# A two-layer decoder trunk on one core: the first loads of x and of the weights put on one DMA queue in the order of their use

## The chip, the core and the metric

The kernel runs on one core of a Trainium2 chip, in one launch. The metric is the time of one execution on the device in microseconds (us); less is better.

## The reference, cut to what matters

The reference is a decoder trunk of two layers (DEPTH = 2) on a sequence of 256 tokens with 1024 features, in float32. Each layer normalises x, projects it once, feeds the parts to three groups of heads, gates their outputs, and adds one output projection to x:

```python
for l in range(DEPTH):
    h = rms_norm(x, g_pre[l])
    u = h @ w_in[l]
    (qa, ka, va, ga, qb, kb, vb, gb, rb, qm, gm) = jnp.split(u, split_idx, axis=-1)
    oa = merge_heads(moba_attention(qa_h, ka_h, split_heads(va, A_HEADS))) * jax.nn.silu(ga)
    ob = merge_heads(rms_norm(ob, g_gla_out[l])) * jax.nn.silu(gb)
    mkv = rms_norm(mem, g_mem[l]) @ w_mem_kv[l]
    om = merge_heads(mem_attention(qm_h, mk_h, split_heads(mv, M_HEADS))) * jax.nn.silu(gm)
    x = x + jnp.concatenate([oa, ob, om], axis=-1) @ w_out[l]
```

Group A is causal attention with eight heads, group B a chunked gated linear attention (GLA) with four heads, group M attention into 256 memory tokens with four heads. (The lines that make `qa_h`, `ob` and the like are left out here.)

## The kernel before, in words

**Tiling.** x is kept with its features on the 128 partitions: 8 k tiles of 128 x 256. All weights come from DRAM in granules of 8 k tiles of 256 columns (1 MB). Each fp32 operand is split into a high part in the matmul's format (`whi`, `xh`, `oh`, made by ScalarE or GpSimd) and the rest (`wlo`, `xl`, `ol`, made by VectorE), and each product is three matmuls: high by high, and the two mixed ones (L990 to L1005). So ScalarE and VectorE have to split every weight before TensorE can use it.

**The order of the work.** The program is written by a small planner (`Plan`, L47). Every chain of work is a Python generator that asks for an engine, a planned cost and a time before which it can't start; the planner always takes the operation that can start first by its own clock, and the instructions are recorded on each engine in that order. On the chip they run in this order on each engine, each waiting for its inputs. The planner's clock needs to be told when loads land: that is what the numbers in `LANDS` (L36) do. They cause no wait themselves; they decide only in which order the engines' instructions are written. A change in them shifts the choices that come behind.

**The first unit.** The first granules of layer 0 (`vr` and `kq`: values and gate rank, keys and queries of group B) come as one array of 528 columns for each k tile. `start_loads` (L321) issues the loads of x and of these weights in five pieces (`CHUNKS`, L35): k tile 0, k tile 1, then 2 and 3, 4 and 5, 6 and 7. For each piece it issues x on SyncE's queue (L331) and then the weights (L332), on ScalarE's queue for k tiles 0 and 1 and on SyncE's for the rest. `first_x` (L377) splits x, `first_w` (L340) splits the weights (L345 on ScalarE, L347 on VectorE), and `first_sq` (L382) squares and sums x for the norm (L309, L314, L317). `main` (L1032) issues 5 matmuls on zeros ahead of all (`WARM`, L1035), and `first_unit` (L1130) then runs 12 matmuls for each k tile, 6 of 272 columns and 6 of 256.

**Behind it.** `loader` (L353) issues one granule after the other on SyncE's queue, each into one of three raw buffers; the first weights take two of the three and give them back when the last `wlo` of the first unit is done (L351). `split` (L389) makes `whi` (L404) and `wlo` (L406) in four parts of two k tiles, in one of two buffers. Layer 0 then runs the units `ga0`, `va0 va1`, `qa0 ka0`, `mk mv`, `qm`, ... (L25); a unit of two names is done with matmuls of 512 columns (L1005). The unit `mk mv` needs the split memory tokens (`oh`, `ol`) and is led on TensorE by the sum of their squares (L438 over `sqs`, which VectorE adds up in L314 and L317). Between the matmuls of the units stand those of the heads: L880 (logits), L932 (transposes), L947 (probabilities by values), L502 (head norms), and L614 to L732 (GLA). The output projection is matmuls of L998 with `oh` and `ol` in a fixed order of k tiles (`KORD`, L27: 6, 7, 1, 0, 2, ... in layer 0; k tiles 2 and 3 are the last four heads of group A).

Of the kernel before, what the change touches and what calls it, by code (L numbers as in the profile page):

```python
# [16 lines left out]
P = 128  # L17
L = 2
KT = 8
T = 256  # L20
EPS = 1e-6
NPRM = 23
# [6 lines left out]
PAIRK = 0  # L29
SPLIT = 6  # L30
MEMPRIO = 6
WARM = 5
FSQ = 6
STATS = 800
CHUNKS = ((0, 1), (1, 2), (2, 4), (4, 6), (6, 8))  # L35
LANDS = ((3000, 4200), (4300, 4900), (5600, 6800), (7400, 8500), (9200, 10300))  # L36
NB = 528
ENTER, LEAVE, CROSS = 89.0, 189.0, 60.0
SLACK, HOLD = 300.0, 600.0
# [128 lines left out]
def trunk(ctx, tc, xp_d, w0_d, memT_d, wvr_d, win_d, wmkv_d, wout_d, wup_d, cst_d, nb_d, out_d):  # L168
    nc = tc.nc
# [4 lines left out]
    plan = Plan()  # L174
# [15 lines left out]
    xp = big([L * NPRM + KT * T], "xp")  # L190
# [44 lines left out]
    def op(eng, cost, after=0.0, prio=None, table=None, mode="full"):  # L235
        return ("op", [(eng, cost)], after, prio, table, mode)
# [84 lines left out]
    def start_loads():  # L321
        S.activation(warm, ones, AF.Exp)
        got, t0 = yield ("acq", raws, 2)
        raw, hi, lo = (x.rearrange("p a b -> p (a b)")[:, :KT * NB].rearrange("p (k n) -> p k n", n=NB)
                       for x in (raw_t[:, 0:2], whi, wlo))
        done[0, "vk"] = (hi, lo)
        src = w0_d.rearrange("p (k n) -> p k n", n=NB)
        for c, (a, b) in enumerate(CHUNKS):
            tx, tw = LANDS[c]
            xs = slice(L * NPRM + a * T if a else 0, L * NPRM + b * T)  # L330
            nc.sync.dma_start(xp[:, xs], xp_d[:, xs])  # L331
            (nc.scalar if b <= 2 else nc.sync).dma_start(raw[:, a:b], src[:, a:b])  # L332
            plan.spawn(first_x(a, b, tx), 30 - 2 * a)
            plan.spawn(first_w(a, b, tw, raw, hi, lo, got), 29 - 2 * a)
        plan.spawn(first_sq(), 5)
        nc.sync.dma_start(cst, cst_d)
        cst_ev.set(12300)
        nc.sync.dma_start(wup, wup_d)

    def first_w(a, b, t, raw, hi, lo, got):  # L340
# [33 lines left out]
    cst_ev = ev()  # L374
    sq0 = []

    def first_x(a, b, t):  # L377
        for k in range(a, b):
            t1 = yield from split_x(xT, 0, 0, xh, xl, k, t, 30 - 2 * a)
            xev[0][k].set(t1)  # L380
# [649 lines left out]
            wrel[l, nm][k // 2].set(t)  # L1030

    def main():  # L1032
        yield op("P", 4300, 0.0, None, None, "main")
        for j in range(WARM):
            TE.matmul(banks.slots[7][2][:, 0:256], lhsT=zero[:, 0:128], rhs=zero, start=True, stop=True)  # L1035
        idx = {(l, n): i for i, (l, n, _, _) in enumerate(seq)}
        for l in range(L):
# [5 lines left out]
            for unit in UNITS[l] if l == 0 else ("vr", "kq", *UNITS[l]):  # L1043
# [8 lines left out]
                t = 0  # L1052
# [6 lines left out]
                for k, m in order:  # L1059
                    tw = 0  # L1060
                    for x in names:
                        tx = yield ("wait", wts[l, x][k])
                        tw = max(tw, tx)
                    tx = yield ("wait", aev[k])
# [190 lines left out]
```

## Time and profile before

| | us |
|---|---|
| median of three runs | 282.81 |
| the three runs | 282.83, 282.81, 280.1 |
| the profiled execution | 281.19 |
| its span in the profile | 279.4 |

The profile comes from the one profiled execution; its span is 1.79 us shorter than that execution's time. All times below are counted from the start of the span. PE is TensorE's matmuls, DVE is VectorE, ACT is ScalarE, POOL is GpSimd, SP is SyncE; a q behind a name is the engine's own queue of instructions that issue DMAs or wait. A matmul's duration in the profile is that from its start until its results are out, so two neighbours overlap; the step from one start to the next is what a matmul costs.

### The profile page before, as it was taken

To read this page: it belongs to the slowest core of one execution; us is meant where nothing else is said; L and a number is where in the kernel's file an instruction comes from. 1 tells how busy PE (TensorE), PEld (TensorE's weight loads), DVE (VectorE), ACT (ScalarE), POOL (GpSimd) and SP (SyncE) were. 2 spreads that over 40 slices of the span, in tenths; PEclk is the share of its full clock that TensorE was granted. 3 is DMA by queue.
4 is the path that set the end of the run, shared out by engine and by line. 5 is a ranking of instruction groups with operands and counts; after the bars stand their busy time and mean duration, and the time that the engine had idled before them with its cause. 6 is when DMAs were issued, how large, how long until landed. Compare 5 with 4: busy or idle time off the path is not lost.

```text
span 279.4 us, 5773 instructions
## 1 busy us (share of the span) xinstructions
PE 272.0 (97%) x2138; PEld 241.1 (86%) x2138; DVE 229.5 (82%) x568; ACT 193.3 (69%) x430; POOL 89.0 (32%) x111
## 2 busy tenths in 40 slices
PE   8899999799999999999999999999999999999994
PEld 7799788487999997999999886789887888989994
DVE  2899799999888898978999798979986787898631
ACT  4874888777797776967773888759787745956400
POOL 3303394160426424400063318213243730510000
PEclk9999999999999999999999999999999999999999
DMA  7999408560734314343545745228233424151111
GB/s 224 402 361 380 175 0 308 198 246 1 289 107 189 103 72 151 122 168 126 201 160 158 287 151 199 104 82 325 63 135 110 192 108 196 50 196 59 56 56 40
DMA packets 8413, 45.76 MB, mean 164 GB/s; under 512 B 945, under 2 KB 2369, under 8 KB 3393
## 3 DMA queue, kind: packets, MB, share of 16 engines
q1 hardware_dynamic: 8096, 44.85, 43.6%
q10 hardware_dynamic: 288, 0.54, 0.7%
q8 instruction: 17, 0.28, 0.4%
q14 instruction: 12, 0.09, 0.1%
HBM read 44.34 MB, written 1.05 MB: 162 GB/s over the span
## 4 chain that ended last, share of the span: by engine, by line
PE 87%; DVE 7%; DMA 2%; ACT 1%; issue 1%
PE bank L998 49%; PE bank L1005 21%; PE bank L947 4%; PE bank L932 3%; PE bank L880 3%; DVE wlo L406 2%; DMA raw<-w_dram 2%; PE bank L502 2%; DVE ol L301 1%; PE bank L732 1%; PE bank L621 1%; DVE sqs L317 1%; ACT L539 0%; PE bank L530 0%; DVE el L581 0%
## 5 line engine op out<-in xcount | busy, mean ns | idle before, releaser
L406 DVE TENSOR_TENSOR wlo<-raw,whi 128x512 fp32r<-128x512 f32 (+1 forms) x144 | 97.8, 700 | 12.0 <-ACT whi L404 10.1
L404 ACT ACTIVATE whi<-raw 128x512 fp32r<-128x512 f32 (+1 forms) x144 | 86.4, 625 | 24.3 <-PE bank L998 11.3
L998 PE MATMUL bank<-xh,whi 128*128 128x256 f32 x160 | 47.1, 294 | 0.0
L998 PE MATMUL bank<-xl,whi 128*128 128x256 f32 x160 | 44.6, 279 | 0.0
L998 PE MATMUL bank<-xh,wlo 128*128 128x256 f32 x160 | 44.6, 279 | 0.0
L917 POOL TENSOR_SCALAR pe<-pe,rc 128x256 f32<-128x256 f32 (+1 forms) x48 | 29.4, 626 | 35.4 <-DVE rc L914 35.2
L998 PE MATMUL bank<-oh,whi 128*128 128x256 f32 x128 | 35.8, 280 | 0.0
L998 PE MATMUL bank<-ol,whi 128*128 128x256 f32 x128 | 35.7, 279 | 0.0
L998 PE MATMUL bank<-oh,wlo 128*128 128x256 f32 x128 | 35.7, 279 | 0.0
L482 POOL TENSOR_TENSOR cc<-ss,nhalf 128x8 f32<-128x8 f32 x12 | 20.5, 1717 | 45.4 <-DVE ss L480 40.9
L1005 PE MATMUL bank<-whi,xh 128*128 128x512 f32 x80 | 32.9, 411 | 0.0
L1005 PE MATMUL bank<-wlo,xh 128*128 128x512 f32 x80 | 31.4, 393 | 0.0
L998 PEld LDWEIGHTS bank<-xh,whi 128*128 128x128 f32 x160 | 30.2, 189 | 1.4 <-issue 1.0
L1005 PE MATMUL bank<-whi,xl 128*128 128x512 f32 x80 | 31.3, 392 | 0.0
L998 PEld LDWEIGHTS bank<-xl,whi 128*128 128x128 f32 x160 | 30.2, 189 | 0.1
L998 PEld LDWEIGHTS bank<-xh,wlo 128*128 128x128 f32 x160 | 30.1, 188 | 0.0
L998 PE MATMUL bank<-whi,xh 128*128 128x256 f32 (+1 forms) x96 | 28.6, 298 | 0.5 <-ACT whi L345 0.5
L998 PE MATMUL bank<-wlo,xh 128*128 128x256 f32 (+1 forms) x96 | 27.6, 288 | 0.5 <-DVE wlo L347 0.4
L998 PE MATMUL bank<-whi,xl 128*128 128x256 f32 (+1 forms) x96 | 27.3, 284 | 0.0
L998 PEld LDWEIGHTS bank<-oh,whi 128*128 128x128 f32 x128 | 24.3, 190 | 0.2 <-issue 0.2
L998 PEld LDWEIGHTS bank<-ol,whi 128*128 128x128 f32 x128 | 24.0, 188 | 0.0
L998 PEld LDWEIGHTS bank<-oh,wlo 128*128 128x128 f32 x128 | 24.0, 188 | 0.0
(188 smaller groups left out, 608.7 us busy)
## 6 DMA issues: line engine op xcount, KB each, us to landing
raw<-win_dram SPq DMA_DIRECT2D x23, 1024.0 KB, 5.3
raw<-wout_dram SPq DMA_DIRECT2D x8, 1024.0 KB, 4.8
raw<-wmkv_dram SPq DMA_DIRECT2D x4, 1024.0 KB, 4.8
raw<-memT_dram SPq DMA_DIRECT2D x2, 1024.0 KB, 4.8
raw<-w_dram SPq DMA_DIRECT2D x3, 528.0 KB, 8.0
raw<-wvr_dram SPq DMA_DIRECT2D x1, 1088.0 KB, 4.9
nb<-nb_dram SPq DMA_DIRECT2D x1, 1024.0 KB, 8.4
out_dram<-xp SPq DMA_DIRECT2D x8, 128.0 KB, 1.9
```

The costliest lines, as they stand in the source:

```text
L301: V.scalar_tensor_tensor(lo[:, k], src[:, k], col(l, g0 + k), hi[:, k].bitcast(F32), op0=ALU.mult, op1=ALU.subtract)
L317: V.tensor_tensor(sqs, sqs, sq[:, j], op=ALU.add)
L404: S.activation(hi[:, cs], raw[:, cs], AF.Copy)
L406: V.tensor_sub(lo[:, cs], raw[:, cs], hi[:, cs].bitcast(F32))
L482: G.tensor_tensor(c, ss, nhalf, op=ALU.pow)
L502: TE.transpose(ps[:, m, tt * P:tt * P + P], n[:, tt, m * P:m * P + P], ident)
L880: TE.matmul(bk[hh][2][:, a:b], lhsT=x[ds], rhs=y[ds], start=(j == 0), stop=(j == len(prs) - 1))
L917: G.tensor_scalar(pe[:, hh, a:b], pe[:, hh, a:b], rc[:, hh, qt:qt + 1], 1.0, op0=ALU.mult, op1=ALU.mult)
L932: TE.transpose(bk[0][2][:, dst:dst + P], pe[:, hh, src:src + P], ident)
L947: TE.matmul(po[64 * hh:64 * hh + 64, q0:T], lhsT=vv[:, j, c:c + 64], rhs=pt[:, hh, 256 * j:256 * j + T - q0], start=(j == 0), stop=(j == 1))
L998: TE.matmul(ps, lhsT=a, rhs=b, start=(first and j == 0), stop=(lastk and j == 2))
L1005: TE.matmul(ps, lhsT=a, rhs=b, start=(first and j == 0), stop=(lastk and j == 2))
```

## The change

The table of the first loads is written as eleven entries in the order of their use, each with x or w, its k tiles and the time at which the planner takes it as landed. All are issued on SyncE's queue. The weights of k tiles 2 and 3 become two transfers of 264 KB (one of 528 KB before). The planner's landing times are later than before (12100 for the last weights, 10300 before), as are two other numbers of its clock (the constants at 12800, the matmuls on zeros until 4700), and there are 6 matmuls on zeros.

```diff
-WARM = 5
+WARM = 6
 FSQ = 6
 STATS = 800
-CHUNKS = ((0, 1), (1, 2), (2, 4), (4, 6), (6, 8))
-LANDS = ((3000, 4200), (4300, 4900), (5600, 6800), (7400, 8500), (9200, 10300))
+LOADS = (("x", 0, 1, 3100), ("w", 0, 1, 4300), ("x", 1, 2, 4600), ("w", 1, 2, 5300), ("x", 2, 4, 6000),
+         ("w", 2, 3, 6700), ("w", 3, 4, 7600), ("x", 4, 6, 8300), ("w", 4, 6, 9900), ("x", 6, 8, 10600),
+         ("w", 6, 8, 12100))
...
-        for c, (a, b) in enumerate(CHUNKS):
-            tx, tw = LANDS[c]
-            xs = slice(L * NPRM + a * T if a else 0, L * NPRM + b * T)
-            nc.sync.dma_start(xp[:, xs], xp_d[:, xs])
-            (nc.scalar if b <= 2 else nc.sync).dma_start(raw[:, a:b], src[:, a:b])
-            plan.spawn(first_x(a, b, tx), 30 - 2 * a)
-            plan.spawn(first_w(a, b, tw, raw, hi, lo, got), 29 - 2 * a)
+        for what, a, b, t in LOADS:
+            if what == "x":
+                xs = slice(L * NPRM + a * T if a else 0, L * NPRM + b * T)
+                nc.sync.dma_start(xp[:, xs], xp_d[:, xs])
+                plan.spawn(first_x(a, b, t), 30 - 2 * a)
+            else:
+                nc.sync.dma_start(raw[:, a:b], src[:, a:b])
+                plan.spawn(first_w(a, b, t, raw, hi, lo, got), 29 - 2 * a)
...
-        cst_ev.set(12300)
+        cst_ev.set(12800)
...
-        yield op("P", 4300, 0.0, None, None, "main")
+        yield op("P", 4700, 0.0, None, None, "main")
```

The lines of the changed kernel stand one or two further down than those of the kernel before (L404 becomes L406, L998 becomes L1000).

SyncE's queue at the program's start, before (`xp` is x with the small parameters, `raw` the weights as loaded, `w_dram` the first weights, 528 columns for a k tile); the weights of k tiles 0 and 1 stand on ScalarE's queue:

```order
L331 DMA xp<-xp_dram 128x302
L331 DMA xp<-xp_dram 128x256
L331 DMA xp<-xp_dram 128x512
L332 DMA raw<-w_dram 128x1056
L331 DMA xp<-xp_dram 128x512
L332 DMA raw<-w_dram 128x1056
```

and now:

```order
L332 DMA xp<-xp_dram 128x302
L335 DMA raw<-w_dram 128x528
L332 DMA xp<-xp_dram 128x256
L335 DMA raw<-w_dram 128x528
L332 DMA xp<-xp_dram 128x512
L335 DMA raw<-w_dram 128x528 x2
L332 DMA xp<-xp_dram 128x512
```

The weights of k tiles 0 and 1 have moved in between the pieces of x, ahead of x of k tiles 2 and 3.

VectorE around the first parts of `mk` and `mv`, before (`wlo` is the low part of a weight granule, `sqs_130` the sum of the memory tokens' squares, `el`, `ee` and `wz` are GLA's; counted from layer 0's first granule, the 21st `wlo` is the first row that reads `wlo` here, and the 24th is the second of the four in the last):

```order
L406 TENSOR_TENSOR wlo<-raw,whi 128x512
L581 TENSOR_TENSOR el_132<-b 128x32x4
L317 TENSOR_TENSOR sqs_130<-sqs_130,sq_103 128x256
L601 TENSOR_TENSOR el_131<-el_131,kf 128x8x16
L583 TENSOR_TENSOR el_132<-b 128x32x4
L406 TENSOR_TENSOR wlo<-raw,whi 128x512
L317 TENSOR_TENSOR sqs_130<-sqs_130,sq_103 128x256
L601 TENSOR_TENSOR el_131<-el_131,kf 128x16x8
L581 TENSOR_TENSOR el_132<-b 128x64x2
L406 TENSOR_TENSOR wlo<-raw,whi 128x512 x4
```

and now, from the 21st `wlo` to the 24th, which is the first of the last row:

```order
L408 TENSOR_TENSOR wlo<-raw,whi 128x512
L666 TENSOR_TENSOR wz_133<-qf,ee 128x128
L595 TENSOR_TENSOR wz_134<-el_131,qf 128x128
L318 TENSOR_TENSOR sqs_130<-sqs_130,sq_103 128x256
L302 SCALAR_TENSOR_TENSOR ol<-raw,xp,oh 128x256
L408 TENSOR_TENSOR wlo<-raw,whi 128x512
L670 TENSOR_TENSOR ee<-ee,kf 128x128
L595 TENSOR_TENSOR wz_134<-el_131,qf 128x128
L408 TENSOR_TENSOR wlo<-raw,whi 128x512
L444 TENSOR_SCALAR vx_610<-bank_99 128x2
L408 TENSOR_TENSOR wlo<-raw,whi 128x512 x3
```

The last sum of squares now stands ahead of the 22nd `wlo` (ahead of the 23rd before), and GLA's L601 and the `el_132` rows have moved behind.

TensorE at the start of the unit `mk mv`, before (`sqs_130` as above, `zl` and `ee` are GLA's, `oh` and `ol` the split memory tokens):

```order
L1005 MATMUL bank_99<-whi,xl 128x512
L679 MATMUL bank_92<-zl_135,ee 128x512
L438 MATMUL bank_94<-ones,sqs_130 128x1 x2
L1005 MATMUL bank_95<-whi,oh 128x512
L1005 MATMUL bank_95<-wlo,oh 128x512
```

and now:

```order
L1007 MATMUL bank_97<-whi,xl 128x512
L440 MATMUL bank_99<-ones,sqs_130 128x1 x2
L1007 MATMUL bank_94<-whi,oh 128x512
L1007 MATMUL bank_94<-wlo,oh 128x512
L1007 MATMUL bank_94<-whi,ol 128x512
```

GLA's matmul L679 has moved into the unit, 37 rows further down on TensorE. From the last part of layer 0's output projection on (the last 1113 of TensorE's 1933 instructions, the last 297 of VectorE's 570 and the last 199 of ScalarE's 386) the order is the same in both kernels.

## Rows read from the trace of the kernel before

**Rows 1.** The page, busy time: engine, busy us, share, instructions.

```profile
PE 272.0 (97%) x2138; PEld 241.1 (86%) x2138; DVE 229.5 (82%) x568; ACT 193.3 (69%) x430; POOL 89.0 (32%) x111
```

**Rows 2.** Who waited for whom, PE alone: us in total, times, longest.

```profile
PE bank L438 <- DVE sqs L317: 1.0, 1, 1.0
PE bank L1005 <- DVE wlo L406: 0.7, 1, 0.7
```

**Rows 3.** The chain that ended last, first 20 us: start us, us, what.

```profile
1.59 5.94 DMA raw<-w_dram
...
8.23 0.80 DVE wlo L347
...
9.08 1.73 PE bank L998 x12
```

**Rows 4.** The timeline of PE, first unit: start us, us, engine, line, instruction.

```profile
5.24 0.79 PE L998 MATMUL bank<-whi,xh 128*128 128x272 f32 x1
5.83 0.43 PE L998 MATMUL bank<-wlo,xh 128*128 128x272 f32 x1
6.06 0.43 PE L998 MATMUL bank<-whi,xl 128*128 128x272 f32 x1
...
7.39 0.28 PE L998 MATMUL bank<-xl,whi 128*128 128x256 f32 x1
7.51 0.28 PE L998 MATMUL bank<-xh,wlo 128*128 128x256 f32 x1
...
19.56 0.50 PE L438 MATMUL bank<-ones,sqs 128*128 128x1 f32 x4
```

**Rows 5.** Line L1035, the matmuls on zeros: durations in ns, first and last start.

```profile
L1035 PE MATMUL bank<-ob x10: 634/634/795, 1.2 to 5.2; 128*128 128x256 f32 x10
```

**Rows 6.** The timeline of the queues that issue the first loads.

```profile
1.18 0.86 ACTq L332 DMA_DIRECT2D raw<-w_dram  x2
...
9.44 6.72 SPq L362 DMA_DIRECT2D raw<-win_dram  x3
```

**Rows 7.** Stretches: per engine us busy; then PEclk, DMA share, GB/s.

```profile
2.00:4.00 2.00, 2.00 (x6) 1.55 (x6) 0.26 (x1) 0.72 (x3) 0.83 (x6) 1.00 0.97 274
4.00:8.00 4.00, 3.79 (x17) 3.22 (x15) 1.44 (x4) 1.58 (x4) 0.01 (x1) 1.00 1.00 342
8.00:12.00 4.00, 3.30 (x22) 2.88 (x23) 3.77 (x8) 3.99 (x9) 1.97 (x3) 1.00 1.05 410
```

**Rows 8.** The timeline of ACT and DVE where the last first weights are split.

```profile
13.08 1.18 ACT L345 ACTIVATE whi<-raw 128x528 fp32r<-128x528 f32 x2 [0.33 <-DMA raw<-w_dram]
...
14.49 1.31 DVE L347 TENSOR_TENSOR wlo<-raw,whi 128x528 fp32r<-128x528 f32 x2
```

**Rows 9.** The timeline of PE at the start of the unit mk mv.

```profile
49.10 1.02 PE L679 MATMUL bank<-zl,ee 128*128 128x512 f32 x2
51.16 0.60 PE L438 MATMUL bank<-ones,sqs 128*128 128x1 f32 x4 [1.03 <-DVE sqs L317]
51.62 0.47 PE L1005 MATMUL bank<-whi,oh 128*128 128x512 f32 x1
52.76 0.50 PE L1005 MATMUL bank<-wlo,oh 128*128 128x512 f32 x1 [0.67 <-DVE wlo L406]
```

**Rows 10.** The chain that ended last, in the same place.

```profile
50.76 0.34 DVE sqs L317
51.10 0.20 DVE el L601
...
51.50 1.21 DVE wlo L406 x2
```

**Rows 11.** The timeline of PE and DVE at the end of layer 0.

```profile
121.60 0.87 PE L947 MATMUL bank<-pts,va 128*64 128x256 f32 x8
...
123.43 0.42 DVE L852 TENSOR_TENSOR ol<-of,oh 128x256 fp32r<-128x256 f32 x1 [0.15 <-ACT oh L850]
...
124.57 0.28 PE L998 MATMUL bank<-oh,whi 128*128 128x256 f32 x1
```

## The prediction

> **What bounds the kernel now.** I read the page first: TensorE's matmuls are busy in 97% of the span, VectorE in 82% [rows 1]. Time can be won only where TensorE stands still or runs slowly, so I next read who makes it wait. Behind the first unit there are two such waits: 1.0 us for a sum of squares (L317) and 0.7 us for a `wlo`, once each [rows 2]. The chain that ended last shows the other place: it begins with the weights of k tile 1, which land 5.94 us after their issue, and goes over their `whi` and `wlo` (8.23 to 9.03) to the matmul at 9.08 [rows 3]. The timeline shows the size: the first unit starts at 5.24, its first 12 matmuls are issued by 7.51, and then almost nothing runs until 9.08; the unit is over at 19.56 [rows 3, 4]. From there TensorE is fed until the unit `mk mv`. There it could have gone on at 50.13 (51.16 less the wait of 1.03), but waits for `sqs`, and then until 52.76 for a `wlo` [rows 9]; the chain runs over VectorE alone there [rows 10]. So there are two places, the first k tile and the start of `mk mv`, and the second belongs to VectorE's arrears. Everything behind layer 0 stands in the same order before and after and reads as busy; I leave it as it is.
>
> **The change part by part.**
>
> *One queue.* Before, the weights of k tiles 0 and 1 are issued by ScalarE's queue at 1.18 [rows 6] and run beside what SyncE's queue has sent. Now 0.83 MB (x and weights of k tiles 0 and 1: 128 partitions x (302 + 256 + 2 x 528) x 4 bytes) stand ahead of everything else. By the rates [rows 7], 0.55 MB are moved between 2 and 4 us, and the other 0.28 MB take 0.8 us at 342 GB/s: 4.8. From the last byte to its use there lies at most 1.9 us: all first loads are 3.24 MB, by the same rows they are through at 11.2, and ScalarE takes up the last at 13.08 [rows 8]. So the weights of k tile 1 can be used at 6.7 at the latest, their `whi` is there at 7.4 and `wlo` at 8.1 (0.65 and 0.80 in the chain, overlapping by little).
>
> *The first unit.* A sixth matmul on zeros puts the first real one off by (5.24 - 1.2) / 5 = 0.8 us [rows 4, 5], to 6.05. Its twelve matmuls take 0.23 from start to start until shortly before 7 (5.83 to 6.06) and 0.12 after it (7.39 to 7.51). The clock column says 1.00 (2.4 GHz) for both [rows 7], so it doesn't explain the change, and I take it by its place: three steps of 0.23 and nine of 0.12 end at 7.8. Bounds: all fast 7.5, all slow 8.8. Without a wait for k tile 1 the other 84 matmuls take 84/83 of the 10.48 from 9.08 to 19.56, so 10.6: the unit ends at 18.4 instead of 19.56, **1.1 us** earlier. The cover: weights of k tiles 4 and 5 end the first 2.43 MB, moved by 9.2 and usable by 11.1; TensorE needs them at 7.8 + 4 x 1.5 = 13.8 less the splits (1.3). For k tile 6 it is 13.08 + 1.25 against 15.3. If the cover goes, each microsecond of a late landing beyond it costs one.
>
> *Two transfers instead of one.* SyncE has three more issues, at 0.4 each (0.86 for ScalarE's two, [rows 6]); the queue runs far ahead of the data, so I take nothing. Bounds: 0 and 1.2 us on everything behind. The rows of those weights are half as long; the rate in the stretch of short ones is 274 GB/s, in that of long ones 410 [rows 7]. The nearest rows are those of 4 to 8 us at 342, where both run. I take the last landing as it is, 13.08, because the bytes are the same and the queue for them too.
>
> The Trainium skill speaks against this edit: its page "DMA: Bandwidth & Descriptors", section "Bandwidth", says to gather transfers to 1 MB or more, with 341 GB/s measured at 1 MB and 138 at 64 KB. The trace agrees as far as its stretches of smaller and larger transfers go (274 and 410 GB/s). By the rule the loads would run at the lower of the rates, which is the slower rival below; by the row of 4 to 8 us they keep their time.
>
> *VectorE up to `mk mv`.* The last first weights are taken up at 13.08; their first `whi` is there at 13.7 (half of 1.18 later) and now nothing stands in VectorE's way: both `wlo` are done at 13.7 + 1.31 = 15.0, against 15.8 [rows 8]: 0.8 earlier. From the last two L347 to the 24th `wlo` (the first of `mv`) VectorE has 79 instructions now, 89 before: three sums of squares went ahead, into time in which it waited (0.34 each), eight of GLA went behind (L581, L583, L593, L601, L670, 0.20 each), one of 0.1 came in [rows 10]: 1.0 + 1.6 - 0.1 = 2.5. So the 24th `wlo` comes 3.3 earlier than 52.71 [rows 10], at 49.4.
>
> *TensorE at `mk mv`.* The GLA matmul at 49.10 [rows 9] now comes later, inside the unit. TensorE is at the sum of squares at 49.10 - 1.1 = 48.0; that sum is ready (it stands ahead of the 22nd `wlo`). It starts `mk mv` at 48.4 (51.16 to 51.62 before) and needs the 24th `wlo` at 48.7, but gets it at 49.4. So it goes on at 49.4 instead of 52.76, 3.3 earlier, and still has the moved matmul to do, which took 1.03 (49.10 to 50.13): **2.3 us** in all, of which 1.1 is the start. Bounds here: 0, if VectorE's lead goes into new waits on the way (only the longest single wait of its kind, 1.03, is then lost again), and 0.7 more, if the `wlo` is in time.
>
> *The end of layer 0.* Two pairs of heads of the last four now finish side by side, with L947 after 18 matmuls of the output projection, and 6 of them ahead of the first use of the first pair's output. Before, one pair has 18 behind it: L947 ends at 122.4, `ol` at 123.85, and its first use is at 124.57 [rows 11]. The chain of 1.45 is now covered by the second pair's L947 (0.8) and six matmuls (0.7), and for the second pair by twelve (1.4). I take 0; bounds -0.3 (TensorE's order has eight groups of matmuls fewer in layer 0) and +1.4 (a chain uncovered).
>
> **The sum.** 281.19 - 2.3 = 278.9 from the profiled execution. It lies 1.6 below the median of the runs; the mean of the four known times is 281.7, and I set the forecast against that: **279.4 us**, 0.8% less.
>
> **The rivals.**
>
> *More.* VectorE's arrears melt further and the `wlo` is there when TensorE wants it: 2.3 + 0.7 + 0.3 = 3.3, so 278.4. For it speaks that three places of VectorE's work went into idle time; against it, that ScalarE has the same table loads and splits to do.
>
> *The start alone.* The 1.1 is won, but the new order of layer 0 gives the rest back, at `mk mv` or in the uncovered chain at the layer's end: between 281.7 - 1.1 = 280.6 and, with the 1.4 of the bound, 282.0. For it speaks that TensorE reads as 97% busy and VectorE has hardly any slack in 15 to 53 us; against it, that VectorE has 2.5 us less to do ahead of the place that waits.
>
> *Slower.* The one queue carries the pieces of 128 to 528 KB at the 274 GB/s of the first stretch [rows 7]. Then 3.24 MB take 11.8 us from 2.0 on and the last weights are usable at 15.7 instead of 13.1. K tile 6 waits 1.2 and the first unit ends at 19.6, no earlier than before. The next granule, which stands behind on the same queue [rows 6], is usable 3.9 later, at 19.6, and split at 20.9: TensorE waits again for 1.2. VectorE is some 3.6 later than forecast, the 24th `wlo` comes at 53.0, and the moved GLA matmul follows: 281.7 + 1.3 = 283.0. From a landing of the last weights at about 14.8 on, the change loses. Against it speaks that six of the eight k tiles were on this queue before too.
>
> *It doesn't do what it says.* The first weights could land no earlier because what holds them up is not the other queue. Then k tile 1 is waited for as before and the sixth matmul on zeros only fills the wait: 281.7 less what VectorE's new order gives, about 280.5.
>
> **How the numbers follow.** The forecast has 0.50, more 0.18, the start alone 0.18, slower 0.07, no earlier landing 0.07. One per cent is 2.8 us, about what a measurement of this kernel can tell from no change. Faster by over that: the rival "more" and some 4 in 10 of the forecast's own spread (the bounds of the first k tile and of `mk mv`, about 1 us to each side), 0.38. Slower by over 1% needs the slower rival with the uncovered chain on top: 0.05. The rest, 0.57, is within. The range reaches from 277.0 (the larger gain, on an execution as short as the profiled one with a further 0.9) to 281.9 (the start alone); what is left out is the slower rival and the last edge of "more".
>
> **What would show it.** Right: the first real matmul at about 6.1 with no gap between k tiles 0 and 1, the first unit over at 18.4, `mk mv` going on at 49.4, and the last 157 us of the span as long as before. Wrong: ScalarE taking up the last first weights later than 14; a wait of more than 1 us at `mk mv` or ahead of L998 at the end of layer 0; a step of 0.23 between matmuls beyond 7 us.

## The result and the profile after

| | before | after |
|---|---|---|
| median of the comparison, 22 executions each | 280.97 | 282.62 |
| lowest to highest | 280.1 to 282.83 | 280.9 to 284.32 |
| profiled execution / its span | 281.19 / 279.4 | 283.19 / 281.3 |

The changed kernel takes 1.0053 of the time before, with an interval of 1.0032 to 1.0074: 1.5 us more. The forecast was 279.4, the range ended at 281.9; sign and range were both missed. Three executions of the experiments below took 537.93, 541.5 and 685.29 us and are left out of all ratios and counts as slow.

The page and the waits of TensorE, of the changed kernel, answer to [rows 1, 2]:

```profile
PE 273.8 (97%) x2140; PEld 242.2 (86%) x2140; DVE 228.9 (81%) x571; ACT 193.0 (69%) x427; POOL 88.5 (31%) x111
```

```profile
PE bank L1007 <- DVE wlo L408: 1.8, 1, 1.8
PE bank L1037 <- DVE ones L1167: 1.2, 1, 1.2
PE bank L1000 <- DVE wlo L349: 0.5, 2, 0.3
PE bank L440 <- DVE sqs L318: 0.3, 1, 0.3
```

TensorE is busy 1.8 us longer with the same matmuls and one more on zeros, and the two waits that should have shrunk (1.0 and 0.7) have become 0.3 and 1.8. A longer busy time for the same work asks for the clock. Stretches of the changed kernel (columns as in [rows 7]; the seventh is the granted clock):

```profile
2.00:4.00 2.00, 2.00 (x6) 1.55 (x6) 0.48 (x1) 0.71 (x2) 0.83 (x6) 1.00 0.94 296
4.00:8.00 4.00, 3.66 (x20) 3.09 (x18) 2.01 (x5) 2.60 (x6) 0.63 (x1) 1.00 0.92 295
8.00:12.00 4.00, 3.82 (x29) 3.61 (x30) 4.00 (x9) 3.13 (x7) 1.66 (x2) 1.00 1.02 363
50.00:52.00 2.00, 0.21 (x2) 0.07 (x1) 2.00 (x7) 2.00 (x7) 2.00 (x2) 1.00 0.70 180
52.00:54.00 2.00, 2.00 (x7) 1.64 (x8) 2.00 (x4) 1.27 (x3) 2.00 (x3) 0.74 1.04 381
54.00:56.00 2.00, 2.00 (x6) 1.52 (x6) 2.00 (x6) 0.00 (x0) 0.73 (x1) 0.50 0.87 352
56.00:58.00 2.00, 2.00 (x10) 1.61 (x9) 1.35 (x6) 0.75 (x2) 1.89 (x2) 0.91 1.04 430
```

Two readings. The bytes of 4 to 8 us went at 295 GB/s, where the profile before had 342. And after 50 to 52 us, in which TensorE ran 0.21 of 2 us, the granted clock fell: 0.74, then 0.50 (1.2 GHz), then 0.91. The timeline of TensorE there, against [rows 9]:

```profile
49.12 0.61 PE L440 MATMUL bank<-ones,sqs 128*128 128x1 f32 x4 [0.31 <-DVE sqs L318]
49.65 0.50 PE L1007 MATMUL bank<-whi,oh 128*128 128x512 f32 x1
51.93 0.50 PE L1007 MATMUL bank<-wlo,oh 128*128 128x512 f32 x1 [1.79 <-DVE wlo L408]
52.27 0.39 PE L1007 MATMUL bank<-whi,ol 128*128 128x512 f32 x1
52.50 0.39 PE L1007 MATMUL bank<-whi,oh 128*128 128x512 f32 x1
...
52.96 0.61 PE L1007 MATMUL bank<-whi,ol 128*128 128x512 f32 x1
53.37 0.63 PE L1007 MATMUL bank<-whi,oh 128*128 128x512 f32 x1
...
55.92 0.60 PE L1007 MATMUL bank<-whi,oh 128*128 128x512 f32 x1
56.35 0.41 PE L1007 MATMUL bank<-wlo,oh 128*128 128x512 f32 x1
```

`mk mv` starts earlier than before (49.65 against 51.62) and goes on only 0.83 earlier (51.93 against 52.76), with the GLA matmul of 1.03 still ahead of it. Then eight steps from 52.96 to 56.35 take 3.39 us, 0.42 each, where 0.23 each would make 1.84: 1.55 us lost at the lower level of the clock. TensorE had stood still just before; whether that is why the clock fell is tested below.

VectorE made it stand still. The timeline where the gate of GLA is made (`az`, `z`), first of the kernel before (TensorE and VectorE):

```profile
27.75 0.69 PE L530 MATMUL bank<-az,wup 16*128 16x256 f32 x2
...
30.74 0.69 DVE L406 TENSOR_TENSOR wlo<-raw,whi 128x512 fp32r<-128x512 f32 x1 [0.75 <-ACT whi L404]
...
32.47 0.42 DVE L541 SCALAR_TENSOR_TENSOR z<-z,az 128x256 f32<-128x256 f32 x1 [1.04 <-ACT az L539]
```

and of the changed kernel, three engines in order of time:

```profile
28.20 0.40 DVE L527 COPY az<-bank 16x256 f32<-16x256 f32 x1
...
30.04 0.69 PE L532 MATMUL bank<-az,wup 16*128 16x256 f32 x2
...
30.77 0.48 ACT L534 ACTIVATE z<-bank,xp 128x256 f32<-128x256 f32 x1 [1.22 <-PE bank L532]
...
33.91 0.43 DVE L543 SCALAR_TENSOR_TENSOR z<-z,az 128x256 f32<-128x256 f32 x1 [3.63 <-ACT az L541]
```

TensorE's gate matmul (L532) now stands behind 18 matmuls of `va0 va1`, at 30.04; before it stood behind six of them, at 27.75. ScalarE's chain over `z` and `az` follows, and VectorE, whose instructions run in the order in which they are written, stands still for 3.63 us ahead of L543. Before, it waited 1.04 there (L541) and 0.75 for a `whi` shortly ahead. That is 1.8 us more of idle time on the engine that was to be 3.3 ahead.

The first unit, in the timeline of TensorE against [rows 4]:

```profile
5.64 0.48 PE L1000 MATMUL bank<-whi,xh 128*128 128x272 f32 x1
5.96 0.29 PE L1000 MATMUL bank<-wlo,xh 128*128 128x272 f32 x1
...
8.01 0.40 PE L1000 MATMUL bank<-wlo,xh 128*128 128x272 f32 x1 [0.35 <-DVE wlo L349]
...
9.90 0.39 PE L1000 MATMUL bank<-wlo,xh 128*128 128x272 f32 x1 [0.17 <-DVE wlo L349]
...
19.33 0.50 PE L440 MATMUL bank<-ones,sqs 128*128 128x1 f32 x4
```

and the timelines of GpSimd and VectorE in the changed kernel, where the last wait of that unit comes from, against [rows 8]:

```profile
12.16 1.27 POOL L262 TENSOR_SCALAR xh<-xp 128x256 fp32r<-128x256 f32 x1 [1.43 <-DMA xp<-xp_dram]
...
13.46 0.49 DVE L302 SCALAR_TENSOR_TENSOR xl<-xp,xh 128x256 fp32r<-128x256 f32 x1 [0.39 <-POOL xh L262]
13.86 0.70 DVE L349 TENSOR_TENSOR wlo<-raw,whi 128x528 fp32r<-128x528 f32 x1
...
14.88 1.32 DVE L349 TENSOR_TENSOR wlo<-raw,whi 128x528 fp32r<-128x528 f32 x2
```

The first real matmul is at 5.64 (5.24 before) and runs fast from 5.96 on (from 6.74 before). But TensorE waits for the `wlo` of k tiles 1, 2 and 5, the last from 14.26 to 14.62: that `wlo` (13.86) stands behind an `xl` of the last k tiles which waits for GpSimd's `xh`, as that had waited for its x. The unit is over at 19.33, 0.23 earlier than before, and the last first `wlo` at 16.2 (14.88 + 1.32), 0.4 later than before (15.8).

### The profile page after: what moved, and what is told of

Its sections match the earlier page's. It is cut to its first block, busy times and chain, and to the rows that moved or that the text cites. A ratio compares the mean times of both kernels' runs of the same rounds, so it can differ in the third digit from the quotient of the medians.

```text
span 281.3 us, 5791 instructions
## 1 busy us (share of the span) xinstructions
PE 273.8 (97%) x2140; PEld 242.2 (86%) x2140; DVE 228.9 (81%) x571; ACT 193.0 (69%) x427; POOL 88.5 (31%) x111
## 4 chain that ended last, share of the span: by engine, by line
PE 81%; DVE 11%; DMA 2%; ACT 2%; SPq 1%; issue 1%; POOL 0%; ACTq 0%
PE bank L1000 43%; PE bank L1007 22%; DVE wlo L408 4%; PE bank L882 3%; PE bank L949 3%; PE bank L934 3%; DMA xp<-xp_dram 2%; PE bank L504 2%; DVE ol L302 1%; PE bank L734 1%; PE bank L623 1%; SPq L335 1%; DVE sqs L318 1%; PE bank L681 1%; SPq L332 1%
## 5 line engine op out<-in xcount | busy, mean ns | idle before, releaser
L408 DVE TENSOR_TENSOR wlo<-raw,whi 128x512 fp32r<-128x512 f32 (+1 forms) x144 | 98.5, 708 | 13.1 <-ACT whi L406 10.7
L406 ACT ACTIVATE whi<-raw 128x512 fp32r<-128x512 f32 (+1 forms) x144 | 86.5, 625 | 27.4 <-PE bank L1000 9.3
L1000 PE MATMUL bank<-xh,whi 128*128 128x256 f32 x160 | 46.4, 290 | 0.0
L1000 PE MATMUL bank<-xl,whi 128*128 128x256 f32 x160 | 44.6, 278 | 0.0
L1000 PE MATMUL bank<-xh,wlo 128*128 128x256 f32 x160 | 44.5, 278 | 0.0
L919 POOL TENSOR_SCALAR pe<-pe,rc 128x256 f32<-128x256 f32 (+1 forms) x48 | 27.8, 594 | 40.1 <-DVE rc L916 39.9
L1000 PE MATMUL bank<-oh,whi 128*128 128x256 f32 x128 | 36.1, 282 | 0.0
L1000 PE MATMUL bank<-ol,whi 128*128 128x256 f32 x128 | 35.8, 279 | 0.1
L1000 PE MATMUL bank<-oh,wlo 128*128 128x256 f32 x128 | 35.7, 279 | 0.0
L484 POOL TENSOR_TENSOR cc<-ss,nhalf 128x8 f32<-128x8 f32 x12 | 21.2, 1768 | 37.6 <-DVE ss L482 29.7
L1000 PEld LDWEIGHTS bank<-xh,whi 128*128 128x128 f32 x160 | 30.1, 188 | 1.0 <-issue 0.7
L1000 PEld LDWEIGHTS bank<-xl,whi 128*128 128x128 f32 x160 | 30.2, 189 | 0.1
L1000 PEld LDWEIGHTS bank<-xh,wlo 128*128 128x128 f32 x160 | 30.1, 188 | 0.0
L1000 PE MATMUL bank<-whi,xh 128*128 128x256 f32 (+1 forms) x96 | 28.2, 294 | 0.0
L1000 PE MATMUL bank<-wlo,xh 128*128 128x256 f32 (+1 forms) x96 | 27.4, 286 | 0.6 <-DVE wlo L349 0.5
L1000 PE MATMUL bank<-whi,xl 128*128 128x256 f32 (+1 forms) x96 | 27.1, 282 | 0.0
L1000 PEld LDWEIGHTS bank<-oh,whi 128*128 128x128 f32 x128 | 24.3, 190 | 0.3 <-issue 0.2
L1000 PEld LDWEIGHTS bank<-ol,whi 128*128 128x128 f32 x128 | 24.0, 188 | 0.3 <-DVE ol L854 0.3
L1000 PEld LDWEIGHTS bank<-oh,wlo 128*128 128x128 f32 x128 | 24.0, 188 | 0.0
```

The costliest lines, as they stand in the source:

```text
L406: S.activation(hi[:, cs], raw[:, cs], AF.Copy)
L408: V.tensor_sub(lo[:, cs], raw[:, cs], hi[:, cs].bitcast(F32))
L484: G.tensor_tensor(c, ss, nhalf, op=ALU.pow)
L919: G.tensor_scalar(pe[:, hh, a:b], pe[:, hh, a:b], rc[:, hh, qt:qt + 1], 1.0, op0=ALU.mult, op1=ALU.mult)
L1000: TE.matmul(ps, lhsT=a, rhs=b, start=(first and j == 0), stop=(lastk and j == 2))
```

## The experiments

Twelve more runs were made, ten of new kernels and one more each of the kernel before and the changed one, always beside the kernel before on the same chip; the ratios are against those runs. Three batches on three chips put the kernel before at 281.15, 281.31 and 280.98.

**The transfers alone, and the order alone.** The first kernel has the eleven transfers of the change on SyncE's queue, and all else (landing numbers, 5 matmuls on zeros, the order on the other engines) as before:

```diff
+        for what, a, b in ISSUE:
+            if what == "x":
+                xs = slice(L * NPRM + a * T if a else 0, L * NPRM + b * T)
+                nc.sync.dma_start(xp[:, xs], xp_d[:, xs])
+            else:
+                nc.sync.dma_start(raw[:, a:b], src[:, a:b])
...
-            nc.sync.dma_start(xp[:, xs], xp_d[:, xs])
-            (nc.scalar if b <= 2 else nc.sync).dma_start(raw[:, a:b], src[:, a:b])
```

> The transfers of the changed kernel (all on SyncE's queue, order of use, k tiles 2 and 3 apart) with the instruction order, the landing numbers and the five matmuls on zeros of the kernel before. Theory (the loss comes from the new order of layer 0 that the planner's numbers deal): the gap between k tiles 0 and 1 (7.6 to 9.1 us) shrinks, the first unit ends 0.5 to 1.2 us earlier than 19.56, nothing else moves: 0.3 to 1.2 us faster than before. Rival (one queue moves the loads more slowly, 295 instead of 342 GB/s in 4 to 8 us, and this costs the time): no gap removed or later splits, 1 to 2 us slower than before.

The second has the order and the numbers of the change, with the five pairs of transfers and the two queues of before.

> The planner's numbers of the changed kernel (landing times, constants, six matmuls on zeros, 4700), so its instruction order on the compute engines, with the transfers of the kernel before (weights of k tiles 0 and 1 on ScalarE's queue, 2 and 3 as one). Theory (new order is the loss): 1.5 to 3.5 us slower than before, with VectorE idle for 3 us or more ahead of L543, a wait of about 2 us for wlo at the start of mk mv and a granted clock under 1.0 behind it. Rival (the one queue is the loss): within 0.7 us of before.

Measured: the transfers alone 281.73 us, ratio 1.0013 (0.9983 to 1.0043); the order alone 282.99, 1.006 (1.0026 to 1.0094). So the loss belongs to the order, and the transfers bring nothing that shows. For the transfers alone neither the theory (0.3 to 1.2 us faster) nor the rival (1 to 2 us slower) came; for the order alone the theory did, with a wait of 3.64 us for the gate and of 1.86 for the `wlo`. In the profile of the first kernel `mk mv` goes on at 51.44, 1.3 earlier than before, and then the clock falls there too. TensorE's timeline and stretches of the run with the transfers alone:

```profile
49.83 0.61 PE L443 MATMUL bank<-ones,sqs 128*128 128x1 f32 x4 [1.14 <-DVE sqs L319]
...
51.44 0.50 PE L1010 MATMUL bank<-wlo,oh 128*128 128x512 f32 x1 [0.67 <-DVE wlo L411]
```

```profile
52.00:54.00 2.00, 2.00 (x8) 0.81 (x6) 2.00 (x6) 0.65 (x2) 0.71 (x1) 0.54 0.54 123
54.00:56.00 2.00, 2.00 (x44) 1.56 (x46) 1.50 (x5) 0.50 (x2) 0.72 (x1) 0.60 0.98 393
```

Each execution also carries its mean granted clock, and this splits them into two groups. The 93 executions of the kernel before in the three batches: 52 at 1.000 with a median of 280.4, 41 at 0.991 to 0.994 with a median of 282.1. With the transfers alone 8 of 12 are at 0.994 or below, with the order alone 6 of 11 (the profiled one is not among these). The 22 executions of the changed kernel in the comparison of the result split in the same way: 16 at 0.988 to 0.994 with a median of 282.9, 6 at 0.999 with 281.3. So a fall of the clock worth about 1.7 us comes in some executions and not in others, of the kernel before too; and the changed kernel is some 0.9 us longer in its executions without a fall as well (281.3 against 280.4, on other chips).

**Is it the standing still at `mk mv` that costs the clock?** The third kernel is the changed one with eight matmuls of 512 columns, whose result nobody reads, ahead of the sum of squares of `mk mv` in layer 0:

```diff
+                if nm == "mv" and l == 0:
+                    for j in range(FILL):
+                        TE.matmul(bk[0][2], lhsT=xh[:, 0, 0:P], rhs=xh[:, 0:2], start=True, stop=True)
```

> The changed kernel with 8 matmuls of 512 columns (xh by xh, into the bank that the unit's first matmul resets) ahead of the sum of squares and the unit mk mv of layer 0; 8 x 0.23 = 1.84 us, in place of a wait of 0.31 + 2.05. Their results are thrown away. Theory (the fall of the granted clock to 0.5 at 53 to 56 us follows from TensorE standing still at 49 to 52): the clock stays at 1.00 there, the matmuls of mk mv keep their step of 0.23, and the time is 1.0 to 1.8 us below that of the changed kernel. Rival (the clock falls by itself, whatever TensorE does there): it falls again, and the time is 0 to 1 us above the changed kernel's.

Measured: 281.5, ratio 1.0013 (0.9988 to 1.0038), against 1.0053 without them; none of the 11 executions is below a mean clock of 0.997. That is the theory's gain (1.1 us by the ratios), with VectorE's wait of 3.63 still there. The same eight matmuls in the kernel with the transfers alone and in the kernel before:

> The transfers of the change with the instruction order of before, and 8 extra matmuls of 512 columns (about 1.9 us) ahead of the sum of squares of mk mv in layer 0, whose output nobody reads. Theory (TensorE standing still at the start of mk mv is what makes its clock fall in many executions, and the first unit does end 1.4 us earlier with these transfers): the extra matmuls lie in the time in which TensorE waits anyway, the granted clock stays at 1.00 between 50 and 60 us, and the 1.3 us that the run without them lost there come back: 279.5 to 280.5, 0.2 to 0.6% less than before, with the executions closer together. Rival A (the fillers only add work; the clock has another cause): 0.5 to 1.5 us more than without them, 282.3 to 283.2. Rival B (the earlier start is eaten by VectorE's arrears whatever the clock does): as before, 281.0 to 281.7, with a wait for wlo that remains at mk mv.

> The kernel before with the same 8 extra matmuls ahead of the sum of squares of mk mv in layer 0. Theory: before, too, lost time to a fall of the clock in about half of its executions (those above 281.2); with the wait filled, nearly all executions lie at 280.1 to 281.0, the median 0.1 to 0.4% less than before. Rival A (the extra matmuls cost their own time): 282.0 to 283.0. Rival B (the spread of before has another cause, such as the landing of the first loads): as before, 281.0, spread from 280 to 283 as before.

Measured: 280.83, ratio 0.9991 (0.9969 to 1.0012), and 280.32, ratio 0.9976 (0.9947 to 1.0004). The median of the second is where the theory put it; but its executions still run from 279.62 to 281.74 at mean clocks of 0.998 to 1.000, so the fall is not the whole spread. The first lies between the theory and its rival B: the clock stayed, and `mk mv` goes on at 52.31, because the first unit of that execution ended at 19.01 and not at the 18.1 of the run without them. The timeline of TensorE in the kernel before with the extra matmuls (L1062), against [rows 9]:

```profile
47.97 1.99 PE L1062 MATMUL bank<-xh 128*128 128x512 f32 x8
49.79 1.02 PE L680 MATMUL bank<-zl,ee 128*128 128x512 f32 x2
50.65 0.50 PE L439 MATMUL bank<-ones,sqs 128*128 128x1 f32 x4
51.01 0.48 PE L1006 MATMUL bank<-whi,oh 128*128 128x512 f32 x1
51.64 0.50 PE L1006 MATMUL bank<-wlo,oh 128*128 128x512 f32 x1
```

The 1.8 us of extra work lie wholly in the time in which TensorE waits for VectorE: from the end of the unit ahead to the first matmul over `wlo` and `oh` there are 3.67 us (47.97 to 51.64), and before 3.66 (49.10 to 52.76). Over all seven kernels with these matmuls, 1 execution of 82 has a mean clock below 0.997; over the kernel before and the three experiments without them it is 63 of 128. So it is shown that the clock falls because TensorE stands still at `mk mv`; why it does so in some executions and not in others stays open. The Trainium skill, page "TensorE: Matmul & The Clock Gate", section "HAM oscillation — how this bites in real kernels", tells the same of matmuls that wait for DMA: the engine falls back to the lower clock and starts its next piece there. The rows of 50 to 58 us agree as to the fall (0.74, then 0.50), not as to the start: the first steps after the wait still took 0.23 (52.27 to 52.50), and the slow ones began at 52.96.

**The gate's chain.** The changed kernel, with a higher priority in the planner for the copy that the gate matmul reads (L527):

```diff
-        t = yield op("V", vcost(T), t)
+        t = yield op("V", vcost(T), t, 9 if l == 0 else None)
```

> The changed kernel with one priority changed: the copy of the gate's low-rank part (L527, layer 0) gets priority 9, so that TensorE's L532 stands behind 9 matmuls of the unit va0 va1 instead of 18 and two wlo fewer stand ahead of the copy. The rest of layer 0's order is dealt anew behind it. Theory (VectorE's arrears at mk mv come from its wait of 3.6 us for the log of the gate): that wait shrinks to under 2 us, the 24th wlo comes at 50 to 51 instead of 51.9, and the time is 0.7 to 3 us below that of the changed kernel. Rival (VectorE is late by its work and not by that wait): the same wait at mk mv, time within 0.5 us of the changed kernel's.

The timeline of VectorE in that run at L543, and of TensorE at `mk mv`:

```profile
31.86 0.42 DVE L543 SCALAR_TENSOR_TENSOR z<-z,az 128x256 f32<-128x256 f32 x1 [1.28 <-ACT az L541]
...
48.81 0.50 PE L1007 MATMUL bank<-whi,oh 128*128 128x512 f32 x1 [0.80 <-ACT whi L406]
50.57 0.51 PE L1007 MATMUL bank<-wlo,oh 128*128 128x512 f32 x1 [1.25 <-DVE wlo L408]
```

VectorE's wait is 1.28 instead of 3.63, and `mk mv` goes on at 50.57 instead of 51.93. The time is 281.95, ratio 1.0024 (0.9995 to 1.0053), 0.8 us below the changed kernel by the ratios and so just inside the theory: TensorE still waits twice, and in 8 of 12 executions the clock falls. The first batch lets the clock be set aside. Its executions without a fall (a mean clock of 0.997 or more), all on one chip:

| kernel | executions | median us |
|---|---|---|
| before | 18 | 280.2 |
| the transfers alone | 4 | 280.47 |
| the order alone | 5 | 281.61 |
| changed, with the extra matmuls | 11 | 281.5 |
| changed, with the earlier gate | 4 | 280.35 |

So the new order costs 1.3 to 1.4 us with the clock up, and the earlier gate, with the order that is dealt anew behind it, gives 1.2 of it back; its four executions (279.93 to 280.51) all lie below the eleven (280.86 to 282.54). With the extra matmuls as well:

> The changed kernel with the copy L527 at a higher priority in layer 0 (VectorE's wait ahead of L543 was 1.3 instead of 3.6 us with that alone) and the 8 extra matmuls, here between the first weights' wait and the first matmul of mk mv. Theory: both causes of the loss are gone, the clock stays at 1.00 between 50 and 60 us and mk mv goes on at 51.0: 279.8 to 280.6, 0.1 to 0.4% less than before. Rival A (the fillers stand where TensorE no longer waits, so they cost): 281.5 to 282.5. Rival B (the loss sits at the end of layer 0 as well): 280.8 to 281.3.

Measured: 280.59, ratio 0.9984 (0.9967 to 1.0001), at the edge of the theory. Beside the third kernel (1.0013) the earlier gate is worth 0.0029, that is 0.8 us; the two intervals put together make that uncertain by as much.

**How far does one profile speak for others?** The kernel before and the changed kernel, unchanged, were each profiled once more.

> The kernel before, unchanged, profiled a second time to see how far one profile speaks for others. Theory: the landing of the first loads differs by up to 1 us between executions, so the first whi of k tile 1 comes between 6.5 and 7.6 and the span between 278.3 and 280.9. Rival (profiles repeat to 0.2 us): whi of k tile 1 at 7.55 and a span of 279.4 again.

> The changed kernel, unchanged, profiled a second time. Theory (the order of the changed kernel puts the gate's chain late whatever the landings do, and TensorE then stands still at mk mv): VectorE waits 3 to 4 us ahead of L543, TensorE waits 1.5 to 2 us for the wlo of mk mv, and in two of three executions the clock then falls; the first weights are taken up last at 12.4 to 13.4. Rival (the first profile was an unlucky one): a wait under 1.5 us ahead of L543 and mk mv going on before 50.5.

The second profile of the kernel before took 279.62 us, with a span of 277.7. ScalarE's timeline at k tile 1 (7.55 in the first profile, with an idle time of 1.95) and TensorE's at the end of the first unit (19.56 in [rows 4]) and at `mk mv`:

```profile
6.09 0.65 ACT L345 ACTIVATE whi<-raw 128x528 fp32r<-128x528 f32 x1 [0.50 <-DMA raw<-w_dram]
...
18.02 0.50 PE L438 MATMUL bank<-ones,sqs 128*128 128x1 f32 x4
...
51.23 0.50 PE L1005 MATMUL bank<-wlo,oh 128*128 128x512 f32 x1 [0.67 <-DVE wlo L406]
```

Both the `whi` (6.09) and the span lie below the theory's ranges (from 6.5 and from 278.3), so executions differ by more than it allowed: the gap at k tile 1 on which the forecast rests was a late landing in that one execution; with the same two queues the weights can also be there 1.5 us earlier. The waits at `mk mv`, in contrast, are the same in both profiles (0.67 for the `wlo`), so these do repeat. The changed kernel's second profile (281.14, span 279.4) shows what its order costs when the clock does not fall; timeline of VectorE and TensorE:

```profile
33.49 0.42 DVE L543 SCALAR_TENSOR_TENSOR z<-z,az 128x256 f32<-128x256 f32 x1 [3.64 <-ACT az L541]
...
48.75 0.61 PE L440 MATMUL bank<-ones,sqs 128*128 128x1 f32 x4 [0.35 <-DVE sqs L318]
...
51.56 0.50 PE L1007 MATMUL bank<-wlo,oh 128*128 128x512 f32 x1 [1.78 <-DVE wlo L408]
```

The long wait at L543 and that for the `wlo` of `mk mv` are there again to within 0.01 us, that for `sqs` to within 0.04: they belong to the order, not to the execution. The step after the wait is fast here (the clock is 1.00 in both stretches from 52 to 56 us). The spans of the two second profiles, neither with a fall, differ by 1.7 us; at `mk mv` the changed kernel goes on 0.33 later (51.56 against 51.23) and has the GLA matmul of 1.03 still to do, which makes 1.4 of them.

**One queue or two halves?** The transfers of the change with the order of before and the extra matmuls, but k tiles 2 and 3 in one transfer:

```diff
- ... ("x", 2, 4), ("w", 2, 3), ("w", 3, 4), ...
+ ... ("x", 2, 4), ("w", 2, 4), ...
```

> As the run with the transfers of the change, the order of before and the extra matmuls, but the weights of k tiles 2 and 3 are one transfer again. Theory 1 (the two half-long transfers are what makes the first weights land later: the last were taken up at 13.18 and 12.39 with them, at 11.64 to 13.08 before): the last first weights are taken up before 12.3, the first unit ends by 18.4 and the time is 280.1 to 280.5. Theory 2 (the one queue alone does it): 12.4 to 13.4 for the last weights, 18.7 to 19.1 for the end of the unit and 280.6 to 281.0, as with the two halves. Rival (it is chance in the landing): medians of both within 0.2 of 280.5.

The two queues of before with the extra matmuls, but two halves:

```diff
-            (nc.scalar if b <= 2 else nc.sync).dma_start(raw[:, a:b], src[:, a:b])
+            for i, j in ((2, 3), (3, 4)) if a == 2 else ((a, b),):
+                (nc.scalar if b <= 2 else nc.sync).dma_start(raw[:, i:j], src[:, i:j])
```

> The kernel before with the extra matmuls, its two queues kept, but the weights of k tiles 2 and 3 as two transfers. Theory 1 (the halves delay the landings): the last first weights after 12.6, 280.6 to 281.0 instead of 280.3. Theory 2 (the one queue does): as without the halves, the last weights at 11.6 to 12.5 and 280.2 to 280.5.

And the order of the change with the earlier gate, the extra matmuls and the transfers of before:

> The order and the landing numbers of the change with the gate's copy L527 at a higher priority and the extra matmuls (280.59 with the transfers of the change), but with the transfers of before. Theory (the one queue costs 0.3 to 0.5 by later landings): 280.0 to 280.3, no worse than before with the extra matmuls (280.32), and the granted clock at 1.00 from 50 to 60 us. Rival (the transfers make no difference, what is left lies in the order of layer 0): 280.5 to 280.9.

Measured: one queue without halves 281.22, ratio 0.9996 (0.9971 to 1.0022); two queues with halves 280.69, 0.9988 (0.9962 to 1.0014); the order of the change with the old transfers 280.7, 0.9976 (0.9953 to 0.9999). The stretch from 4 to 8 us, first of one queue without halves, then of two queues with them, columns as above:

```profile
4.00:8.00 4.00, 4.00 (x23) 3.64 (x22) 2.75 (x6) 2.75 (x6) 0.92 (x1) 1.00 1.03 350
```

```profile
4.00:8.00 4.00, 3.08 (x18) 2.47 (x16) 1.41 (x5) 1.91 (x5) 0.41 (x1) 1.00 1.01 365
```

None of the three theories is borne out whole. The one queue without halves has the unit over at 18.2, as theory 1 said, but its 281.22 lies above the ranges of both; its profiled execution (279.96) was the shortest of the twelve, so that the row may flatter it. The two queues with halves have the time of theory 1 and the landing of theory 2 (the last weights at 12.52, at its edge). The order of the change with the old transfers keeps the clock at 1.00 from 50 to 60 us, but its 280.7 lies in the rival's range (the transfers make no difference); by the ratio it is as good as the kernel before with the extra matmuls. Over all profiles of the study (orders of both kernels; start of k tile 1's `whi` where ScalarE's row shows it, start of the last first weights' `whi`, and the matmul behind the first unit; one execution each):

| transfers | profiles | GB/s, 4 to 8 us | k tile 1 | last weights | unit over |
|---|---|---|---|---|---|
| two queues, with or without halves | 6 | 342 to 392 | 6.1 to 7.6 | 11.6 to 13.1, mean 12.3 | 18.0 to 19.6, mean 18.9 |
| one queue, halves (the change) | 7 | 282 to 324 | 6.0 to 6.6 | 12.4 to 13.4, mean 12.9 | 18.1 to 19.3, mean 18.8 |
| one queue, no halves | 1 | 350 | 5.8 | 12.4 | 18.2 |

The one queue brings k tile 1 earlier and more evenly. With the two halves it is also slower from 4 to 8 us, and the last weights come 0.6 later in the mean. The unit ends at the same time, to 0.1. Neither the halves on two queues (365) nor the one queue without halves (350) shows the low rate, which speaks for both together; but there is one profile only of each, and the ratio of the one queue is no better without the halves than with them (0.9996 against 0.9991), so which of the two parts costs time, if one does, stays open.

## Why the prediction was wrong

Two terms of the sum failed, and one was missing. The 1.1 us of the first unit rested on one late landing, and 0.1 of it is left. VectorE's lead of 3.3 us, from which the rest of the 2.3 was to come, went in the main into a wait of 3.63 us ahead of L543 (1.79 in all before) that the sum did not have: `mk mv` went on 0.83 earlier, not 3.3. And the sum held the clock at 1.00, which falls at `mk mv` in many executions.

**The base.** The 281.7 that the forecast was set against lies 0.7 above the median of the 22 executions, so the miss is larger than the times show: 2.3 us less forecast, 1.5 more measured. "The first unit": 1.1 us earlier, of the 2.3 in the sum. The 19.56 of [rows 4] was the latest of six profiles with the two queues, whose mean is 18.9; seven with the transfers of the change have 18.8, where the forecast was 18.4. The step that failed is to take a landing from one execution as the kernel's own: 0.1 is left of the 1.1. The weights of k tile 1 usable at 6.7 at the latest was right (6.57), and the sixth matmul on zeros put the first real one off by 0.4 in the first pair of profiles (5.64 against 5.24) and by 0.8, as forecast, in the second (5.86 against 5.08).

**"Two transfers instead of one": nothing taken.** The weighed row of 342 GB/s was kept, and the rate became 295. The Trainium skill's rule (page "DMA: Bandwidth & Descriptors", section "Bandwidth": gather transfers) pointed the right way for this queue: the seven profiles with halves on one queue have 282 to 324, the one without 350. The rule alone does not tell it, since halves on two queues kept 365. The size lies between the forecast and the rival "slower" at 274. In the changed kernel's profile the unit waited for three `wlo`, 1.1 us in all beyond the usual steps of 0.13 (0.71 from 7.30 to 8.01, 0.46 and 0.36), and the last weights came at 13.43, where I had left 13.08. How much of this the rate makes is not shown: the first of the three waits is in the second profile of the kernel before as well (6.87 to 7.54), so it belongs to the splits, and only the last (14.26 to 14.62) goes back to a late load, that of x for GpSimd's `xh`.

**"VectorE up to `mk mv`": 24th `wlo` at 49.4.** It ended at 51.9 (the row of TensorE at 51.93). The count was right (10 instructions fewer, 2.5 us), and it was not what decides: I counted instructions and did not follow what each waits for. The copy for the gate, the gate matmul behind 18 instead of 6 matmuls, and ScalarE's chain put a stall of 3.63 us into VectorE, where there were 1.04 and 0.75. This could have been read from the order ahead of time. Of the 2.5 by which the forecast was missed the stall makes 1.8 (3.63 less 1.79); the other 0.7 is less than the 1.2 by which the first splits ended late (16.2, forecast 15.0).

**"TensorE at `mk mv`": 3.3 earlier, 1.03 given back.** It went on 0.83 earlier, with 1.03 to give back: a loss of 0.2 instead of a gain of 2.3. The bound of 0 here was too narrow, because it knew waits only and not what a wait does to the clock.

**A cost that the sum did not have: the clock.** All rows of before that I used show 1.00, and I took the clock as given. Yet in 41 of 93 executions the kernel before also has the fall, and the profiled one happened to be one without. With a wait of 1.8 us instead of 0.7 ahead of the second matmul it fell in the changed kernel's first profile, for 1.55 us, and not in the second. In the changed kernel it fell in 16 of 22 executions; with the extra matmuls it falls in none of 11, and the ratio goes from 1.0053 to 1.0013.

**"The end of layer 0": 0.** The end of layer 0 in TensorE's timeline of the changed kernel, against [rows 11]:

```profile
122.42 1.86 PE L949 MATMUL bank<-pts,va 128*64 128x256 f32 x16
...
125.14 0.38 PE L1000 MATMUL bank<-oh,whi 128*128 128x256 f32 x1
125.60 0.38 PE L1000 MATMUL bank<-ol,whi 128*128 128x256 f32 x1
```

Both pairs of heads now stand side by side, as read from the order, but the first pair's `ol` comes late (0.46 from 125.14 to 125.60, where such a step behind a break takes 0.2): 0.3 us lost. The term was small, as taken, and inside its bounds.

**What the parts are worth.** From the ratios, in us of 281: the changed kernel +1.5; without the fall of the clock +0.4 (1.0013); with the gate's chain early -0.4 (0.9984); with the old transfers -0.7 (0.9976). The kernel before without its own falls of the clock is at -0.7 as well (0.9976). So of the 1.5 about 0.4 are more frequent or longer falls of the clock (1.1 in the changed kernel less 0.7 in that of before), 0.8 the gate's chain, 0.2 the transfers; the rest of the new order costs and gives nothing that shows. Each of these differences is uncertain by 0.8 to 0.9 us, so of the steps only the one of 1.1, from 1.0053 to 1.0013, is clear of zero. The executions without a fall, on one chip, are sharper and set the gate's chain higher: 1.3 to 1.4 us for the new order, 1.2 of which the earlier gate gives back, and the more frequent falls on top.

**The rivals.** The measured 282.62 lies close to the rival "slower" (283.0), but not for its reason: that rival had the last weights usable at 15.7, and they were at 13.43, and the 24th `wlo` at 53.0, which came at 51.9. Its number is near by luck. "The start alone" names the right place, `mk mv`, where the new order gives the gain back; but the 1.1 that it keeps was not there either. Of the signs of being wrong, the wait of more than 1 us at `mk mv` came, the other two did not.

The last 157 us, said to stay as they are, did. A matmul early in layer 1 (L455 before, L457 after) is at 150.43 before and at 152.14 after: 1.71 of the 1.9 us by which the spans differ were lost ahead of it.

## What to carry to other kernels

Before a forecast is set on a gap at the start of a kernel, profile the same kernel twice: a load's landing moved by 1.5 us here between executions, while waits that come from the order came back to within 0.04 us. Read each execution's mean clock too, and compare executions without a fall with one another: that told the order's 1.3 us from the clock's 1.7 here. When a planner rewrites the order, follow the short chains across engines (a copy, a small matmul, a table load), not the count of instructions on a busy engine: a small matmul that slid behind twelve more large ones took back 1.8 us of the 2.5 that ten instructions fewer had saved. And where TensorE must wait anyway, work that is thrown away can be worth its place, because it keeps the clock: eight unused matmuls put the kernel before at 0.9976 (0.9947 to 1.0004), and the changed order with the earlier gate and the old transfers at 0.9976 (0.9953 to 0.9999). The first interval just includes no change; no kernel of the study has a lower ratio.

## What was not expected of the hardware

The clock fell after stretches in which TensorE still did some work (0.21 of 2 us in the changed kernel; in the run with the transfers alone two waits of 1.1 and 0.7 us came before it), and it did so in one execution and not in the next of the same program. And the first fast matmul of the first unit came at 6.74 in one profile of the kernel before and at 5.65 in the other, both behind the same five matmuls on zeros, while the granted clock of the profile's stretches reads 1.00 for both; the step of 0.23 ahead of it is twice the later 0.12, as 1.2 and 2.4 GHz would make it. So for the first microseconds the steps may tell more than that column; no run here decides it.
